# Two operand sums in other places of VectorE's row, one cast from VectorE to ScalarE, one copy from GpSimd to ScalarE

## The chip, the core and the metric

The kernel runs on one core of a Trainium2 chip. The engines are PE (TensorE, matrix products, with its weight loads PEld), DVE (VectorE), ACT (ScalarE), POOL (GpSimd) and SP (SyncE, which here only issues transfers). Each engine works through its own list of instructions in order and waits for the others by semaphores. The metric is the device time of one launch in microseconds (us). Before the change the median of six runs is 120.89 us (120.22 to 121.39).

## The reference

```python
a: (1024, 1024)   b: (1024, 2048)   c: (2048, 1024)      # float32
h = np.matmul(a, b)
h = 0.5 * h * (1 + np.tanh(np.sqrt(2 / np.pi) * (h + 0.044715 * h ** 3)))
return np.matmul(h, c).astype(np.float32)
```

Two matrix products with a tanh-GELU between them. The hidden matrix h has 1024 rows and 2048 columns.

## The kernel before

The kernel holds the hidden matrix transposed (`hT`, two halves of 512 columns, one for each half of the rows of a), so that the first product needs a transposed: `aT`, made on PE from bfloat16 copies of a. The order of the work on every engine is written out by hand. It has four stages.

**The plain stage (`block`, L136, and `mm1`, L99).** The first 512 columns of b are multiplied in the ordinary way, while a and this part of b arrive. SP loads a in eight pieces (`load_a(h, q)`: half h of the rows, quarter q of the columns) and b in four, alternately: a(0,0), b0, a(1,0), a(0,1), b1, a(1,1), a(0,2), b2, and so on. Each piece of a goes through three steps: `cast_a` (L115) makes a bfloat16 copy `ab` on the engines that it is given, in equal parts; `turn` (L123) transposes its eight 128x128 tiles on PE into a bank of PSUM; and DVE copies the two halves of the bank into `aT` (L129). Pieces of b are cast on ACT (`cast_b`, L131). `block(h, tiles, ks)` then runs the products of half h for contraction steps ks. At the end ACT puts the eight results through GELU.

**Stage zero (`seven(zero, ...)`, L391)** computes the next 512 columns of h as a 2x2 block product with seven block multiplications in place of eight (Strassen-Winograd). Its blocks of a are `BB[k half][row half]` (L200), views of `aT`; its blocks of b are quarters of columns 512 to 1023 of `b1`. The seven products are P1, P2, P5, P6, P7, P4, P3 in the order in which they run here, with 4 contraction steps each and two output tiles each, so 8 matmuls for each product. The operands have to be made first:

- from a, on DVE: `t1` (into `t[0]`), `t2` (into `t[1]`, uses `t[0]`), `t3` (into `t[2]`) and `t4` (into `t4`, uses `t[1]`); `t[3]` is a float32r copy of `BB[1][1]`. `t1(2, 0)` is the first half of the sum (contraction steps 0 and 1 of four), `t1(2, 1)` the second. A half has 1024 elements in each of 128 partitions.
- from b, on DVE: `s1`, `s2` (uses `s1`), `s3`, `s4`; on ACT: `plain_s`, a negated copy.

P5 multiplies `s[0]` by `t[0]`, P6 `s[1]` by `t[1]`, P7 `s[2]` by `t[2]`, P4 `s[3]` by `t4`, and P3 `s4` by `t[3]`. Between the products the function `between0` (L361) puts the remaining sums into the lists: `s3` and `s4` after P2's additions, the two halves of `t4` after those. Results leave PSUM by ACT (`snap`, L277, copies a bank) and DVE (`plus`, L282, adds a bank to such a copy).

**Stage one** does the same for columns 1024 to 2047 with four tiles for each product, from `b2`, and reuses zero's sums of a. **Stage two** is the second product, also with seven multiplications, from `hT` and `c_sb`; it ends with the stores.

The buffers matter for the change. Slots `x0` to `x3` of the pool `big` are used several times. `x1` first holds the float32 quarters 0 and 1 of a (`sta[0]`), `x3` the quarters 2 and 3 (`sta[1]`). Then `pair(1)` puts `t[0]` and `t[1]` into `x1` (L227) and `pair(3)` puts `t[3]` and the home of `s[0]` into `x3` (L256). A write into a slot must wait until all casts have read what was there. `pair(2)` takes `x2`, which nothing uses earlier.

POOL issues the transfers that cast on their way: six of 512 KB for the other three quarters of b (L87, L90: the first two for `b1`, which stage zero needs, then four for `b2`), and eight of 512 KB for c (L259 and L260). They start when a(0,3) is there (`gate`, L82). In the list of POOL the two copies into `t[3]` (L258) stand between b's issues and c's.

Of the kernel before, what the change touches and what calls it, by code (L numbers as in the profile page):

```python
# [19 lines left out]
def kernel(ctx, tc, a, b, c, out):  # L20
    nc = tc.nc
# [5 lines left out]
    NT = N // 128  # L27
# [3 lines left out]
    cv = c.rearrange("(nt p) q -> p nt q", p=128)  # L31
# [8 lines left out]
    def slot(tag, shape, dt, name):  # L40
        return big.tile(shape, dt, name=name, tag=tag)

    def bank(i, shape=(128, H), dt=F32, name="ps"):
        return pp.tile(list(shape), dt, name=name, tag=f"bank{i}", padded_shape=None)

    def pieces(tag, bufs, shape, dt, name):
        return small.tile(shape, dt, name=name, tag=tag, bufs=bufs)
# [8 lines left out]
    c_sb = keep.tile([128, NT, P], BF16, name="c_sb")  # L56
# [31 lines left out]
    for n in range(2):  # L88
        for k in range(0, KT, 4):
            nc.gpsimd.dma_start(out=b2[:, k:k + 4, ts(n, H)],  # L90
                                in_=bv[:, k:k + 4, ds(1024 + n * H, H)])

    def copy(eng, dst, src):
        if eng is nc.scalar:
            nc.scalar.activation(dst, src, AF.Copy)
        else:
            nc.vector.tensor_copy(dst, src)

    def mm1(p, t, h, ks):  # L99
        for k in ks:  # L100
            nc.tensor.matmul(p, b1[:, k, ts(t, 128)], aT[:, h, k],  # L101
                             start=(k == 0), stop=(k == KT - 1))

    def gelu(t, h, p):
        nc.scalar.activation(hT[h][:, t], p, AF.Gelu_apprx_tanh)  # L105
# [9 lines left out]
    def cast_a(h, q, *engs):  # L115

        ab = pieces("ab", 2, [128, 4, 256], BF16, "ab")
        for i, eng in enumerate(engs):
            w = 256 // len(engs)
            copy(eng, ab[:, :, ts(i, w)], sta[q // 2][:, h, q % 2][:, :, ts(i, w)])  # L120
        return ab

    def turn(h, q, i, ab):  # L123
        pt = bank(i, (128, 2, H), BF16, "pt")
        for n in range(2):
            for m in range(4):
                nc.tensor.transpose(pt[:, n, ts(m, 128)], ab[:, m, ts(n, 128)], ident)  # L127
        for n in range(2):
            nc.vector.tensor_copy(aT[:, h, 2 * q + n], pt[:, n])  # L129

    def cast_b(k, n=1):  # L131
        for i in range(n):
            r = ds(i * (H // n), H // n)
            nc.scalar.activation(b1[:, k, r], stb[:, k, r], AF.Copy)  # L134

    def block(h, tiles, ks):  # L136
        for k in ks:
            for t in tiles:
                mm1(ps[h, t], t, h, (k,))
# [56 lines left out]
    def pair(i):  # L196
        x = slot(f"x{i}", [128, 2, 4, H], F32R, "x1")
        return x[:, 0], x[:, 1]

    BB = [[aT[:, 0, 0:4], aT[:, 1, 0:4]], [aT[:, 0, 4:8], aT[:, 1, 4:8]]]  # L200

    def quarters(b, c0, w):
        return [[b[:, 0:4, ds(c0, w)], b[:, 4:8, ds(c0, w)]],
                [b[:, 0:4, ds(c0 + w, w)], b[:, 4:8, ds(c0 + w, w)]]]

    zero = Seven(4, quarters(b1, H, 256), BB, [None] * 4, [None] * 4, 2)
# [11 lines left out]
    ab = cast_a(0, 1, nc.scalar, nc.scalar)  # L218
# [2 lines left out]
    block(1, range(3), (1,))  # L221
    cast_b(2)
    cast_b(3)
    ab = cast_a(1, 1, nc.vector, nc.vector)
    block(0, range(4), (2,))
    turn(1, 1, 7, ab)
    zero.t[0], zero.t[1] = pair(1)  # L227
    zero.t1(2, 0)
    block(0, range(4), (3,))
    ab = cast_a(0, 2, nc.scalar)  # L230
    cast_b(4)
# [4 lines left out]
    ab = cast_a(1, 2, nc.vector)  # L236
# [4 lines left out]
    ab = cast_a(0, 3, nc.scalar)  # L241
# [3 lines left out]
    turn(0, 3, 7, ab)  # L245
    block(1, range(3), (5,))
    ab = cast_a(1, 3, nc.scalar, nc.vector)
    zero.t1(2, 1)
    block(0, range(4), (6, 7))
    for t in range(4):  # L250
        gelu(t, 0, ps[0, t])
    ps[1, 3] = bank(7)
    mm1(ps[1, 3], 3, 1, range(2))
    turn(1, 3, 0, ab)
    mm1(ps[1, 3], 3, 1, range(2, 6))
    zero.t[3], x31 = pair(3)  # L256
    for i in (0, 2):
        nc.gpsimd.tensor_copy(zero.t[3][:, i:i + 2], BB[1][1][:, i:i + 2])  # L258
    for t in range(0, NT, 2):  # L259
        nc.gpsimd.dma_start(out=c_sb[:, t:t + 2], in_=cv[:, t:t + 2])  # L260
    zero.t[2], x21 = pair(2)
    zero.t3(2, 0)
    zero.t2(2, 1)
    zero.t3(2, 1)
    block(1, range(3), (6, 7))
# [95 lines left out]
    def between0(n):  # L361
        if n == "P1":
            zero.plain_s()
        elif n == "P2":
            zero.s3()
            zero.s4(x31[:, :, 256:])
        elif n == "P5":
            zero.t4(t4, 2)
            one.last_t = t4
# [19 lines left out]
    zero.s1()  # L389
    zero.s2()  # L390
    seven(zero, done0, between0)  # L391
    one.s[3] = slot("b1", [128, 2, 4, H], F32R, "x1")[:, 0]
    one.s1()
# [68 lines left out]
```

## Time and profile before

| what | value |
|---|---|
| median of six runs | 120.89 us (120.22 to 121.39) |
| profiled execution: its own time / its span | 121.18 us / 119.4 us |
| PE busy in the span | 112.7 us (94%), 538 matmuls |
| DVE busy | 91.3 us (76%), 106 instructions |
| ACT busy | 55.7 us (47%), 92 instructions |
| POOL busy | 14.0 us (12%), 23 instructions |
| granted clock of PE | 1.00 in all stages |
| plain stage, 0 to 26.64 us | PE 23.92, DVE 14.37, ACT 12.79 us busy |
| stage zero, 26.64 to 40.75 us (14.11 us) | PE 13.40, DVE 12.60, ACT 9.18 us busy |
| stage one, 40.75 to 65.83 us (25.08 us) | PE 25.08, DVE 19.81, ACT 17.79 us busy |
| stage two, 65.83 to 119.40 us (53.57 us) | PE 50.31, DVE 44.54, ACT 15.90 us busy |

The busy time of PE is the sum of modelled spans of pipelined matmuls, so 100% does not mean its peak. The stages are cut where the first matmul of each stage starts. The profiled execution took 1.78 us more than its span: that is what lies around it.

### The profile page before, as it was taken

The numbers are of one execution on the slowest core, as the hardware profiler recorded it, in microseconds if no ns is written. First come the engines' busy times: TensorE is split into PE (matmuls) and PEld (weight loads), VectorE is DVE, ScalarE is ACT, GpSimd is POOL, SyncE is SP. The second block draws the span as 40 slices with busy tenths as digits, with TensorE's granted clock in tenths as the row PEclk, the third lists the DMA queues.
The fourth block names the chain that finished last, engine by engine and source line by source line (L and its number), as shares of the span: only waits on it lengthen the run. The fifth ranks groups of instructions, "written<-read, shape, count | busy, mean of one in ns | idle before, by whom it ended". The sixth has DMA issues, their size and how long they took to land.

```text
span 119.4 us, 1474 instructions
## 1 busy us (share of the span) xinstructions
PE 112.7 (94%) x538; PEld 77.0 (65%) x538; DVE 91.3 (76%) x106; ACT 55.7 (47%) x92; POOL 14.0 (12%) x23
## 2 busy tenths in 40 slices
PE   6698999999998999999999999999999999999990
PEld 5453655444675644888888444488888888888860
DVE  0242497789999599980779999999999986964570
ACT  4046347569275689436669536900032992000000
POOL 2000008969332000000000000000000000000000
PEclk9999999999999999999999999999999999999999
DMA  3999999999999999999000000052000002004993
GB/s 82 291 367 364 365 353 301 184 206 207 207 206 213 210 214 210 213 210 179 3 0 0 0 5 0 0 175 88 0 0 0 0 0 93 0 21 175 365 354 139
DMA packets 13543, 17.91 MB, mean 150 GB/s; under 512 B 737, under 2 KB 8929, under 8 KB 13537
## 3 DMA queue, kind: packets, MB, share of 16 engines
q0 software_dynamic: 5344, 7.34, 35.0%
q1 hardware_dynamic: 8192, 10.49, 25.8%
q8 instruction: 4, 0.07, 0.2%
q14 instruction: 3, 0.02, 0.0%
HBM read 20.97 MB, written 4.19 MB: 211 GB/s over the span
## 4 chain that ended last, share of the span: by engine, by line
PE 81%; DVE 8%; DMA 5%; ACT 2%; issue 1%; SPq 0%; DVEq 0%
PE ps L192 66%; PE ps L101 13%; DVE x L150 6%; DMA stb<-in_b_dram 5%; PE pt L127 3%; ACT hT L105 2%; DVE ot L284 1%; DVE aT L129 0%; SPq L68 0%; DVE ot L350 0%; ACT b L134 0%; DVEq L284 0%
## 5 line engine op out<-in xcount | busy, mean ns | idle before, releaser
L192 PE MATMUL ps<-x,s 128*128 128x512 f32 x128 | 29.6, 391 | 0.0
L192 PEld LDWEIGHTS ps<-x,s 128*128 128x128 f32 x128 | 24.0, 188 | 5.1
L192 PE MATMUL ps<-x,x 128*128 128x512 f32 x96 | 22.7, 392 | 0.3 <-DVE x L150 0.3
L192 PEld LDWEIGHTS ps<-x,x 128*128 128x128 f32 x96 | 17.9, 188 | 4.5 <-ACT x L188 0.7
L101 PE MATMUL ps<-aT,b 128*128 128x512 bf16 x64 | 16.9, 408 | 0.6 <-DVE aT L129 0.5
L192 PE MATMUL ps<-c_sb,hT 128*128 128x512 bf16 (+1 forms) x72 | 14.2, 356 | 0.0
L279 ACT ACTIVATE v<-ps 128x512 f32<-128x512 f32 x10 | 6.0, 598 | 17.4 <-PE ps L192 17.4
L192 PE MATMUL ps<-x 128*128 128x512 f32 x56 | 13.6, 394 | 0.4 <-DVE x L150 0.3
L105 ACT ACTIVATE hT<-ot 128x512 bf16<-128x512 f32 x18 | 10.7, 626 | 5.4 <-DVE ot L284 5.4
L192 PEld LDWEIGHTS ps<-x 128*128 128x128 f32 x56 | 10.2, 188 | 3.5 <-DVE x L150 0.8
L284 DVE TENSOR_TENSOR ot<-ps,v 128x512 f32<-128x512 f32 x10 | 6.7, 688 | 6.4 <-DMA out_dram<-ot 3.9
L192 PEld LDWEIGHTS <-hT 128*128 128x128 bf16 x72 | 6.9, 98 | 7.0 <-issue 0.5
L129 DVE COPY aT<-pt 128x512 bf16<-128x512 bf16 x16 | 6.0, 420 | 7.0 <-PE pt L127 6.9
L101 PEld LDWEIGHTS <-b 128*128 128x128 bf16 x64 | 6.2, 103 | 7.9 <-issue 1.4
L192 PE MATMUL ps<-aT,b 128*128 128x512 bf16 x48 | 10.7, 379 | 0.0
L284 DVE TENSOR_TENSOR ot<-ps,u 128x512 f32<-128x512 f32 x10 | 6.7, 690 | 5.1 <-ACT u L279 5.1
L150 DVE TENSOR_TENSOR x<-c_sb 128x1024 fp32r<-128x1024 bf16 x8 | 9.2, 1218 | 0.0
L105 ACT ACTIVATE hT<-ps 128x512 bf16<-128x512 f32 x14 | 7.3, 596 | 2.1 <-PE ps L101 2.1
L192 PEld LDWEIGHTS <-b 128*128 128x128 bf16 x48 | 4.6, 98 | 5.7 <-issue 0.3
L279 ACT ACTIVATE u<-ps 128x512 f32<-128x512 f32 x10 | 5.9, 598 | 3.3 <-PE ps L192 3.2
L279 ACT ACTIVATE p<-ps 128x512 f32<-128x512 f32 x9 | 5.3, 599 | 3.8 <-PE ps L192 3.8
L134 ACT ACTIVATE b<-stb 128x512 bf16<-128x512 f32 (+1 forms) x9 | 4.7, 573 | 5.0 <-DMA stb<-in_b_dram 5.0
(39 smaller groups left out, 113.4 us busy)
## 6 DMA issues: line engine op xcount, KB each, us to landing
sta<-in_a_dram SPq DMA_DIRECT2D x8, 512.0 KB, 8.9
c_sb<-in_c_dram POOLq DMA_DIRECT2D x8, 512.0 KB, 19.5
b<-in_b_dram POOLq DMA_DIRECT2D x6, 512.0 KB, 10.4
out_dram<-ot SPq DMA_DIRECT2D x12, 256.0 KB, 2.1
stb<-in_b_dram SPq DMA_DIRECT2D x4, 512.0 KB, 8.7
out_dram<-ot SPq DMA_DIRECT2D x8, 128.0 KB, 2.0
```

Source lines behind the costliest of these rows:

```text
L101: nc.tensor.matmul(p, b1[:, k, ts(t, 128)], aT[:, h, k], start=(k == 0), stop=(k == KT - 1))
L105: nc.scalar.activation(hT[h][:, t], p, AF.Gelu_apprx_tanh)
L127: nc.tensor.transpose(pt[:, n, ts(m, 128)], ab[:, m, ts(n, 128)], ident)
L129: nc.vector.tensor_copy(aT[:, h, 2 * q + n], pt[:, n])
L134: nc.scalar.activation(b1[:, k, r], stb[:, k, r], AF.Copy)
L150: nc.vector.tensor_tensor(out=dst[:, r], in0=x[:, r], in1=y[:, r], op=op)
L192: nc.tensor.matmul(p[:, ds(c0, w)], l[:, k, ts(j, 128)], r[:, k, ds(c0, w)], start=(start and k == 0), stop=(k == self.kt - 1), skip_group ...
L279: nc.scalar.activation(st, p, AF.Copy)
L284: nc.vector.tensor_tensor(out=ot, in0=p, in1=st, op=ADD)
```

## The change

Five things are done. The cast of a(1,1) goes from DVE (two instructions) to ACT (two instructions). On DVE `t1(2, 0)` moves ahead of the two copies of `turn(1, 1)`, and `t1(2, 1)` takes the place that `t1(2, 0)` had. `t3(2, 0)` moves to where `t1(2, 1)` was, ahead of the last copies into `aT`. The copy into `t[3]` goes from POOL to ACT in two halves: the first between the two groups of GELUs at the end of the plain stage, the second after `plain_s` in stage zero. And c's eight issues on POOL, with no copy ahead of them any more, follow directly on b's; their lines are now L92 and L93. The number of instructions on PE and its order are the same; the lists of DVE, ACT and POOL change by -2, +4 and -2 instructions.

```diff
@@ -89,6 +89,8 @@
             nc.gpsimd.dma_start(out=b2[:, k:k + 4, ts(n, H)],
                                 in_=bv[:, k:k + 4, ds(1024 + n * H, H)])
+    for t in range(0, NT, 2):
+        nc.gpsimd.dma_start(out=c_sb[:, t:t + 2], in_=cv[:, t:t + 2])
@@ -221,11 +223,12 @@
     cast_b(2)
     cast_b(3)
-    ab = cast_a(1, 1, nc.vector, nc.vector)
+    ab = cast_a(1, 1, nc.scalar, nc.scalar)
     block(0, range(4), (2,))
-    turn(1, 1, 7, ab)
     zero.t[0], zero.t[1] = pair(1)
     zero.t1(2, 0)
+    turn(1, 1, 7, ab)
+    zero.t1(2, 1)
     block(0, range(4), (3,))
     ab = cast_a(0, 2, nc.scalar)
@@ -245,21 +248,17 @@
     block(1, range(3), (5,))
     ab = cast_a(1, 3, nc.scalar, nc.vector)
-    zero.t1(2, 1)
+    zero.t[2], x21 = pair(2)
+    zero.t3(2, 0)
     block(0, range(4), (6, 7))
     for t in range(4):
         gelu(t, 0, ps[0, t])
+    zero.t[3], x31 = pair(3)
+    zero.plain_t(2, 0)
     ps[1, 3] = bank(7)
     mm1(ps[1, 3], 3, 1, range(2))
     turn(1, 3, 0, ab)
     mm1(ps[1, 3], 3, 1, range(2, 6))
-    zero.t[3], x31 = pair(3)
-    for i in (0, 2):
-        nc.gpsimd.tensor_copy(zero.t[3][:, i:i + 2], BB[1][1][:, i:i + 2])
-    for t in range(0, NT, 2):
-        nc.gpsimd.dma_start(out=c_sb[:, t:t + 2], in_=cv[:, t:t + 2])
-    zero.t[2], x21 = pair(2)
-    zero.t3(2, 0)
     zero.t2(2, 1)
     zero.t3(2, 1)
     block(1, range(3), (6, 7))
@@ -361,6 +360,7 @@
         if n == "P1":
             zero.plain_s()
+            zero.plain_t(2, 1)
```

## The prediction

> **What bounds the kernel now.** I read the stage table first. Stage one has no gap on PE (25.08 us busy of 25.08), stage zero has one: 13.40 of 14.11. PE's timeline says where, and its waits say on whom.
>
> ```profile
> 26.64 3.62 PE L192 MATMUL ps<-aT,b 128*128 128x512 bf16 x16
> 30.53 3.87 PE L192 MATMUL ps<-x,x 128*128 128x512 f32 x16 [0.27 <-DVE x L150]
> 34.24 2.86 PE L192 MATMUL ps<-x 128*128 128x512 f32 x10
> 37.43 3.47 PE L192 MATMUL ps<-x 128*128 128x512 f32 x14 [0.34 <-DVE x L150]
> ```
>
> The columns are start, length, engine, line, operation, count, idle time and releaser. Both stops wait for DVE's sums. The listed idle times are too small, since ends are modelled; I work with starts. In P1 and P2 (16 matmuls) the first starts at 26.64 and the last ends at 30.26; with some 0.39 for one, the starts are (3.62 - 0.39)/15 = 0.215 apart, so P5 could have begun at 26.64 + 16 x 0.215 = 30.08. It began at 30.53: **0.45 lost**. P5 and P6 take (34.24 - 30.53)/16 = 0.232 each. Ten matmuls follow (8 of P7, 2 of P4), so the third of P4 could have begun at 34.24 + 10 x 0.232 = 36.56. It began at 37.43, five hundredths after the end of t4's second half (37.38): **0.87 lost**. Together 1.32 us.
>
> Stage one follows at 40.75. What DVE did in that time is the second view, with POOL's row beside it.
>
> ```profile
> 24.25 0.76 DVE L129 COPY aT<-pt 128x512 bf16<-128x512 bf16 x2 [1.06 <-PE pt L127]
> 24.92 1.22 DVE L150 TENSOR_TENSOR x<-aT 128x1024 fp32r<-128x1024 bf16 x1
> 26.06 2.06 DVE L150 TENSOR_TENSOR x<-aT,x 128x1024 fp32r<-128x1024 bf16 x1
> 28.04 1.21 DVE L150 TENSOR_TENSOR x<-aT 128x1024 fp32r<-128x1024 bf16 x1
> 29.17 1.21 DVE L150 TENSOR_TENSOR x<-b 128x1024 fp32r<-128x1024 bf16 x1
> 30.42 1.23 DVE L150 TENSOR_TENSOR x<-x,b 128x1024 fp32r<-128x1024 f32 x1
> 31.56 1.28 DVE L284 TENSOR_TENSOR ot<-ps,p 128x512 f32<-128x512 f32 x2
> 32.76 1.22 DVE L150 TENSOR_TENSOR x<-b 128x1024 fp32r<-128x1024 bf16 x1
> 33.89 1.22 DVE L150 TENSOR_TENSOR x<-b,x 128x1024 fp32r<-128x1024 bf16 x1
> 35.03 2.35 DVE L150 TENSOR_TENSOR x<-x,aT 128x1024 fp32r<-128x1024 f32 x2
> ```
> ```profile
> 25.07 1.97 POOL L258 CAST x<-aT 128x1024 fp32r<-128x1024 bf16 x1 [0.92 <-DVE aT L129]
> 26.99 3.65 POOL L260 DMA_DIRECT2D c_sb<-in_c_dram  x5
> ```
>
> From the last copy into aT on, DVE has no idle time: t3(2,0), t2(2,1), t3(2,1), s1, s2, two additions, s3, s4, t4. So whatever leaves this row ahead of s1 moves everything behind it, and P5 (needs s1) and P4 (needs t4) are what PE stops for. One sum is odd: t2's second half took 2.06, its first half, same form, 1.23 at 19.80. POOL's copy ran until 27.04 beside it.
>
> From 37.43 on the chain of waits is PE alone up to the last addition:
>
> ```profile
> 37.43 78.72 PE ps L192 x358
> 116.16 0.02 issue
> 116.18 0.42 DVE ot L350
> ```
>
> so time won before 37.43 reaches the end, if nothing later stands at a fixed time.
>
> **The change, part by part.**
>
> *t3(2,0) leaves the row behind 24.25.* It goes to 21.98, where t1's second half stood (1.22, the same length); t1's second half goes to 15.66, where its first stood, and the first to 13.67, where DVE ran the two casts of a(1,1) (0.75 for both). What is left behind 24.25 is shorter by 26.06 - 24.92 = 1.14.
>
> *POOL's copies go.* t2(2,1) should take 1.23 as its first half did: its distance to the next sum falls from 1.98 to 1.14, 0.84 less. Bounds: 0 (the stretch has another cause) and 0.84; I take 0.84, since POOL's record ends at 27.04, 1.08 before t2's end, about what is left of a sum.
>
> *A dependence appears:* t2(2,1) now follows directly on the copy that it reads. s2 behind s1 shows such a distance: 30.42 is 0.04 after s1's end (30.38), where free sums overlap by 0.08. So it starts 0.04 after the copies' end (25.01), at 25.05 and not at 24.92: 0.13 lost.
>
> DVE's row is thus earlier by 1.14 + 0.84 - 0.13 = 1.85 from t3(2,1) on: t2(2,1) at 25.05, t3(2,1) 26.19, s1 27.32, s2 28.57, additions 29.71 and 30.31, s3 30.91, s4 32.04, t4 33.18 to 35.53. Each must find its inputs. s1 reads the second of b's chunks: issued at 19.4, landed 7.6 later at 27.0, by the issue and landing times. P2's two tiles end at about 29.4 and 30.26, just ahead of their additions.
>
> *PE then:* P5 at 30.08 (s1 done 28.53); P6 at 31.94 (s2 done 29.80); P7 at 33.79 (s3 done 32.13); P4 at 35.65 (t4's first half done 34.40), its third matmul at 36.11 (second half done 35.53). Nothing waits, with 0.58 to spare at the last: 1.32 won. Since 0.58 is spare, small errors in the 1.85 don't matter.
>
> *The cast of a(1,1) on ACT* costs two of the row of a(0,1)'s, 1.15 for both. ACT was idle from 12.15 to 14.07. When does a(1,1) land? These ACT rows tell:
>
> ```profile
> 11.00 1.15 ACT L134 ACTIVATE b<-stb 128x512 bf16<-128x512 f32 x2 [0.16 <-DMA stb<-in_b_dram]
> 14.07 1.06 ACT L95 ACTIVATE ab<-sta 128x1024 bf16<-128x1024 f32 x1 [1.92 <-DMA sta<-in_a_dram]
> ```
>
> b1 is there at 11.00 and a(0,2) at 14.07, with a(1,1) between them; a(1,3) came 1.50 after b3 (19.73, 21.23). So about 12.5, and the cast ends at 13.65. There is a new wait: t1(2,0) writes slot x1, which this cast reads, so DVE stands until the cast is done, and behind it stand the copies of turn(1,1) at 14.99. DVE is free for it at 13.7; t1 then ends at about 14.95. No cost, but no reserve above some 0.1. Bounds: 0, and with a landing only just before 13.67 (where DVE's cast began without waiting) t1 would start at 14.86 and end at 16.08, 1.0 late. I take 0. The second half of t1 reads the copy ahead of it and starts some 0.1 later than 15.66; DVE had 16.88 to 16.94 idle ahead of the next copies, so at most some hundredths reach PE.
>
> *The two copies on ACT* take 1.05 each, as plain_s (same size) does. The first lies in the idle 24.79 to 25.98 between the GELU groups, 0.14 to spare. Without that cover the four GELUs and P1's snaps behind them would slip as much as it overran; the second snap ends at 29.16, and the second addition needs it at 30.31. The second goes 30.11 to 31.16; then the two GELUs (1.23) to 32.4, and P6's first snap is due at 33.53 less 0.45, 33.08. No cost; 0.7 spare.
>
> *c's eight issues* pass POOL's copies and start at 23.09 in place of 26.99. Nothing lands earlier: in one queue the last b chunk ends at 37.3 (22.4 + 14.9), and from the third issue on each waits for a b chunk in both kernels. c is first used at 63.45, the last of it has landed at 37.5 + 20 = 57.5. Cost 0. The Trainium skill speaks against early issues (SBUF — State Buffer, SBUF: two separate sides): while VectorE runs certain fast copies, GpSimd can't write the descriptors of its transfers. The rows show four issues of 0.745 (20.12 to 23.09) beside DVE casts and copies, 0.71 each with sums alone; by the rule an issue at 24.25 would stand for up to the 0.76 of the copies, by the rows for 0.04, and in both cases the queue is full until 37.3, so the sum stays.
>
> **Sum:** 121.18 - 0.45 - 0.87 = 119.86 for the profiled execution (span 118.1). That execution lay 0.29 above the median, so the median goes from 120.89 to **119.6**. Its own range is 119.2 to 120.1: 0.3 of scatter, and partial costs.
>
> **Rivals.**
> 1. *Only part of it is won.* If t2's stretch stays, 0.84 - 0.58 = 0.26 comes back: 119.8. If P4's weights waited for ACT's snap u, as the releaser in PEld's row at 36.36 says, 0.38 stays (36.48 in place of 36.10): 120.0. Against the second: the snap ended at 36.02, t4's first half at 36.25.
> 2. *a(1,1) comes late*, and 1.0 is lost in the plain stage: 120.6. Against: the 1.50 between b3 and a(1,3).
> 3. *Eaten later:* in stage two DVE has hardly a gap from 63 to 97, and t3 ends (92.57) as P7 starts; if this row doesn't move along, 120.9. Against: it starts behind an addition at 61.45 that waited for PE, so it moves with PE.
> 4. *Slower: c's transfers share with b's.* If the engines served several chunks of the queue in turn, the second b chunk, alone 2.5 us, would share with two of c's and land up to 5 us later, at 32. P2 (28.36) and s1 would stand: 3.6 more, 124.5. It is slower from a landing 2 us late on (29.0, as s1 began at 29.17). Against: with five of c's issued from 26.99 on, b's chunks still ended 2.5 apart (POOL's waits end at 32.46, 34.96, 37.49).
>
> **How the numbers follow.** Forecast 0.66; rival 1 0.10; rival 2 0.08; rival 3 0.08; rival 4 and its like 0.08. A measurement of this kernel tells 0.5% (0.6 us) from no change. Faster: 0.66 + 0.10 + half of rival 2 = 0.80. Same: 0.04 + 0.08 = 0.12. Slower 0.08. The range goes to 120.7, which takes in rival 2, and down to 119.1.
>
> **What would show it.** Right: P5 starts 16 x 0.215 after P1, no wait of PE on DVE in stage zero, t2(2,1) at 1.2, stage one at about 39.4, later stages of the same length. Wrong: a wait of PE on aT between 14 and 19, a matmul of P2 that waits for b, or a longer stage two.

## The result

| | before | after |
|---|---|---|
| median | 120.67 us (120.22 to 121.39, 38 runs) | 119.87 us (119.68 to 120.11, 17 runs) |
| ratio | | 0.9923 (95%: 0.9906 to 0.9939) |
| profiled execution: time / span | 121.18 / 119.4 us | 119.71 / 117.9 us |
| first matmul of stage zero | 26.64 us | 26.54 us |
| length of stage zero | 14.11 us | 12.73 us |
| length of stage one | 25.08 us | 25.08 us |
| length of stage two | 53.57 us | 53.55 us |

The kernel became faster, by 0.0077 x 120.67 = 0.93 us (0.74 to 1.13); the medians themselves lie 0.80 apart. 119.6 was predicted, with a gain of 1.32 us. A run more than 1.5% above the fastest of its kernel counts as slow and stands in no median or ratio here. The two profiled executions differ by 1.47 us, more than the medians: this is the riddle of the case. Where the time went is plain from the two traces. Stage zero lost 1.38 us, the other stages stayed as they were.

PE's timeline of the changed kernel in stage zero (start, length, engine, line, operation, count):

```profile
26.54 3.62 PE L194 MATMUL ps<-aT,b 128*128 128x512 bf16 x16
29.81 4.00 PE L194 MATMUL ps<-x,x 128*128 128x512 f32 x16
33.65 5.78 PE L194 MATMUL ps<-x 128*128 128x512 f32 x24
39.27 7.08 PE L194 MATMUL ps<-aT,b 128*128 128x512 bf16 x32
```

Both stops are gone: P7, P4 and P3 are one piece of 24 matmuls. DVE's timeline of the same execution:

```profile
13.79 1.22 DVE L152 TENSOR_TENSOR x<-aT 128x1024 fp32r<-128x1024 bf16 x1 [1.57 <-ACT ab L97]
14.93 0.75 DVE L131 COPY aT<-pt 128x512 bf16<-128x512 bf16 x2
...
24.94 1.22 DVE L152 TENSOR_TENSOR x<-aT,x 128x1024 fp32r<-128x1024 bf16 x1
26.09 1.22 DVE L152 TENSOR_TENSOR x<-aT 128x1024 fp32r<-128x1024 bf16 x1
27.69 1.23 DVE L152 TENSOR_TENSOR x<-b 128x1024 fp32r<-128x1024 bf16 x1 [0.39 <-ACT hT L107]
...
33.56 2.35 DVE L152 TENSOR_TENSOR x<-x,aT 128x1024 fp32r<-128x1024 f32 x2
```

t2's second half takes 1.22 in place of 2.06. s1 (27.69) is idle for 0.39 first. The releaser named there, a GELU of ACT, is hardly what it waits for: s1 reads the second chunk of b, whose landing the trace puts at 19.4 + 8.0 = 27.4; POOL's fourth issue of c, which the trace has waiting for that transfer, starts at 27.68; and in two later runs the idle time ahead of s1 is put down to the transfer. t4 ends at 35.91; the third matmul of P4 needs it at about 33.65 + 10 x 0.234 = 35.99. The reserve of 0.58 in the prediction was 0.08.

The riddle shows at the start. PE's timelines, first of the kernel before, then of the changed kernel:

```profile
7.13 3.48 PE L101 MATMUL ps<-aT,b 128*128 128x512 bf16 x8
...
14.34 0.61 PE L127 MATMUL pt<-ident,ab 128*128 128x128 bf16 x8
```
```profile
7.02 1.90 PE L103 MATMUL ps<-aT,b 128*128 128x512 bf16 x8 [0.70 <-ACT b L136]
...
13.29 0.92 PE L129 MATMUL pt<-ident,ab 128*128 128x128 bf16 x8 [0.33 <-ACT ab L97]
...
15.40 0.81 PE L103 MATMUL ps<-aT,b 128*128 128x512 bf16 x3 [0.33 <-DVE aT L131]
```

The same 8 products took 3.48 us in one execution and 1.90 in the other: 0.43 and 0.215 apart. (0.43 is called half pace from here on, 0.215 full pace.) The second execution was through with the products ahead of the transposes of a(1,1) at 12.96, had to wait there, and began them 1.05 us earlier than the first. The chain of waits of the changed kernel names on what:

```profile
3.65 8.85 DMA sta<-in_a_dram
...
12.60 1.16 ACT ab L97 x2
13.76 0.02 issue
13.79 1.22 DVE x L152
15.01 0.35 DVE aT L131
15.36 0.04 issue
15.40 0.81 PE ps L103 x3
```

a(1,1) lands at 12.5, ACT casts it, t1's first half waits for that cast, the copies into aT wait for t1, PE waits for the copies.

### The profile page after: what moved, and what is told of

Its sections match the earlier page's. It is cut to its first block, busy times and chain, and to the rows that moved or that the text cites. A ratio compares the mean times of both kernels' runs of the same rounds, so it can differ in the third digit from the quotient of the medians.

```text
span 117.9 us, 1471 instructions
## 1 busy us (share of the span) xinstructions
PE 110.6 (94%) x538; PEld 75.9 (64%) x538; DVE 90.0 (76%) x104; ACT 58.6 (50%) x96; POOL 11.0 (9%) x21
## 4 chain that ended last, share of the span: by engine, by line
PE 84%; DMA 8%; SPq 2%; DVE 2%; ACT 1%; issue 0%; ACTq 0%
PE ps L194 75%; PE ps L103 8%; DMA sta<-in_a_dram 8%; PE pt L129 2%; SPq L68 1%; SPq L72 1%; DVE x L152 1%; ACT ab L97 1%; DVE ot L349 0%; DVE aT L131 0%; ACTq L97 0%
## 5 line engine op out<-in xcount | busy, mean ns | idle before, releaser
L103 PE MATMUL ps<-aT,b 128*128 128x512 bf16 x64 | 15.6, 379 | 1.6 <-DVE aT L131 0.8
L194 PE MATMUL ps<-aT,b 128*128 128x512 bf16 x48 | 10.7, 379 | 0.0
L97 ACT ACTIVATE ab<-sta 128x512 bf16<-128x512 f32 (+1 forms) x7 | 5.0, 747 | 5.0 <-DMA sta<-in_a_dram 5.0
L152 DVE TENSOR_TENSOR x<-b 128x1024 fp32r<-128x1024 bf16 (+1 forms) x4 | 7.0, 1751 | 0.4 <-ACT hT L107 0.4
```

Source lines behind the costliest of these rows:

```text
L103: nc.tensor.matmul(p, b1[:, k, ts(t, 128)], aT[:, h, k], start=(k == 0), stop=(k == KT - 1))
L152: nc.vector.tensor_tensor(out=dst[:, r], in0=x[:, r], in1=y[:, r], op=op)
L194: nc.tensor.matmul(p[:, ds(c0, w)], l[:, k, ts(j, 128)], r[:, k, ds(c0, w)], start=(start and k == 0), stop=(k == self.kt - 1), skip_group ...
```

## The experiments

Two theories were put up. **Theory S**: the start of PE decides. The kernel before's executions are of two kinds, with PE at half pace until about 10.5 us or at full pace from 5.4 us on, and the profiled one was of the first kind; the kernel before gains from an early PE, the changed one is held by the cast of a(1,1). **Theory D**: the start does not matter; c's earlier transfers delay b's second chunk, and that costs what is missing.

**Dummy matmuls at the start: more, and fewer.**

```diff
-    stir(256, 256, 256, 128)
+    stir(256, 256, 256, 128, 128, 64)     # before_warm, after_warm
+    stir(256, 256)                        # before_cold, after_cold
```

before_warm: 

> The kernel before with two more dummy matmuls (128 and 64 columns) ahead of the first transposes, which fill PE's idle time from 4.5 to 5.5 us; nothing else. Theory S (the start of PE decides: in the profiled execution of before, PE ran its first 8 products 0.43 us apart until 10.5 us, in that of after 0.215 apart): more executions start at full pace, so the median goes from about 120.7 to the lower group of before's times, 120.3 to 120.6, and the profile shows the first 8 products in about 1.9 us and stage zero starting at 26.0 to 26.2. Theory D (the start does not matter; what is missing is lost because c's early transfers delay b's second chunk): 120.5 to 120.9 with the same spread as before.

after_warm: 

> The changed kernel with the same two more dummy matmuls. Theory S: it is held in the plain stage by the cast of a(1,1) and the sum behind it, not by PE's pace, so 119.7 to 119.9 as without them, 0.7 below before_warm. Theory D: as the changed kernel too, 119.9, but 0.8 or more below before_warm.

before_cold: 

> The kernel before with two of the four dummy matmuls (256 columns each) at the start, so that PE is idle from about 3.1 to 5.5 us. Theory S: nearly all executions start at half pace, as in the profiled one; 121.1 to 121.6. Theory D: 120.6, no more than 0.2 from before.

after_cold: 

> The changed kernel with the same two dummy matmuls. Theory S: PE then comes to the transposes of a(1,1) at about 14.3, after the cast on ACT, so the prediction's sum applies: 1.2 to 1.4 below before_cold, 119.9 to 120.3. Theory D: 0.8 to 0.9 below before_cold.

The runs of the unchanged kernel before beside these gave 120.60. before_warm: 120.63 (120.43 to 121.46), ratio 1.0011 (0.999 to 1.0033). after_warm: 119.79 (119.62 to 120.18), 0.9924 (0.9895 to 0.9953). before_cold: 121.23 (120.27 to 121.92), 1.0045 (1.0021 to 1.0069). after_cold: 120.23 (119.80 to 121.38), 0.9967 (0.9943 to 0.9991).

As a switch the extra matmuls did nothing that can be seen: 9 of 12 runs of before_warm lie below 120.8, 26 of the 31 of the kernel before beside them. But the profile of before_warm caught what the profile of before did not, an execution with PE at full pace (time 120.47):

```profile
7.01 1.90 PE L101 MATMUL ps<-aT,b 128*128 128x512 bf16 x8 [0.51 <-ACT b L134]
...
25.93 3.62 PE L192 MATMUL ps<-aT,b 128*128 128x512 bf16 x15
29.82 3.91 PE L192 MATMUL ps<-x,x 128*128 128x512 f32 x16 [0.27 <-DVE x L150]
33.57 2.82 PE L192 MATMUL ps<-x 128*128 128x512 f32 x10
36.73 3.47 PE L192 MATMUL ps<-x 128*128 128x512 f32 x14 [0.34 <-DVE x L150]
40.04 6.22 PE L192 MATMUL ps<-aT,b 128*128 128x512 bf16 x27
```

before_cold's profile is one at half pace (time 121.21):

```profile
7.05 3.59 PE L101 MATMUL ps<-aT,b 128*128 128x512 bf16 x8 [0.41 <-ACT b L134]
...
26.68 3.62 PE L192 MATMUL ps<-aT,b 128*128 128x512 bf16 x16
...
40.78 5.57 PE L192 MATMUL ps<-aT,b 128*128 128x512 bf16 x24
```

Stage zero is equally long in both (14.11, 14.10), and both stops are there. Only its start moves, by 0.75, and the time with it, by 0.74. So the kernel before has two times, about 120.5 and 121.2, by PE's pace at the start: its 38 runs lie in two groups (20 up to 120.67, 15 from 121.08, three between), and fewer dummy matmuls put 9 of 12 into the upper one, against 5 of the 31 beside them. That each of these runs belongs to its group by PE's pace is inferred; three profiled executions show it. Theory S holds for the kernel before. The changed kernel, at full pace, starts stage zero at 26.54, where before at full pace starts it at 25.93: its plain stage is 0.61 longer, stage zero 1.38 shorter, sum 0.77; the times differ by 120.47 - 119.71 = 0.76. DVE's lines show where the 0.61 arises. In before_warm the copies of turn(1,1) stand at 13.85, in the changed kernel behind t1's first half, at 14.93:

```profile
13.85 0.76 DVE L129 COPY aT<-pt 128x512 bf16<-128x512 bf16 x2 [0.49 <-PE pt L127]
```

after_cold doesn't settle its part: 1.00 below before_cold lies between the theories. In its profile (121.38) the first piece of b came to ACT 1.13 late (7.68 in place of 6.55) and the half pace lasted through the transposes behind the products (1.06 for eight, 0.66 in before_cold's). Less the 1.13 its time would be 120.25, about the median, so half pace that lasts longer may be what after_cold's executions have in common; one profile doesn't show it.

**c's transfers late.** A one-column copy on POOL, which waits for the last part of aT, stands ahead of c's issues.

```diff
-    for t in range(0, NT, 2):
-        nc.gpsimd.dma_start(out=c_sb[:, t:t + 2], in_=cv[:, t:t + 2])
...
+    nc.gpsimd.tensor_copy(g2, BB[1][1][:, 3, 0:1])
+    for t in range(0, NT, 2):
+        nc.gpsimd.dma_start(out=c_sb[:, t:t + 2], in_=cv[:, t:t + 2])
```

> The changed kernel with c's transfers issued only when the last part of aT is there (a copy of one column on POOL ahead of them), some 2 us later. The prediction costs their earlier issue at nothing: 119.8 to 119.9, and b's second chunk lands at 27.5 to 27.8 here too. If the early issues delay that chunk (theory D): it lands at 27.0 to 27.2, s1 starts at 27.3, and the time is the same or up to 0.1 less.

Measured 119.98 (119.79 to 120.27), ratio 0.9915 (0.9884 to 0.9947). c's first issue began at 26.24 in place of 23.06, and s1 waits for b's second chunk as ever. DVE's line of c_late:

```profile
27.94 1.23 DVE L151 TENSOR_TENSOR x<-b 128x1024 fp32r<-128x1024 bf16 x1 [0.54 <-DMA b<-in_b_dram]
```

Theory D falls. In the traces whose loads began as usual that chunk lands between 27.0 and 27.8, with late c's (27.0 in before, 27.5 in before_warm, 27.7 in before_cold, 27.1 in pool_back, 27.6 in c_late) and with early ones (27.4 in the changed kernel, 27.5 in after_warm, 27.8 in order, 27.2 in both). That spread belongs to the executions, not to the change.

**One part undone at a time.** pool_back puts the copy into `t[3]` back on POOL, with c's issues behind it as before, t3_back puts t3's first half back behind the last copies into aT, plain_back undoes what the change does in the plain stage.

```diff
-    for t in range(0, NT, 2):                         # pool_back
-        nc.gpsimd.dma_start(out=c_sb[:, t:t + 2], in_=cv[:, t:t + 2])
...
-    zero.plain_t(2, 0)
...
+    for i in (0, 2):
+        nc.gpsimd.tensor_copy(zero.t[3][:, i:i + 2], BB[1][1][:, i:i + 2])
+    for t in range(0, NT, 2):
+        nc.gpsimd.dma_start(out=c_sb[:, t:t + 2], in_=cv[:, t:t + 2])
...
-            zero.plain_t(2, 1)
```
```diff
-    zero.t[2], x21 = pair(2)                          # t3_back
-    zero.t3(2, 0)
...
     mm1(ps[1, 3], 3, 1, range(2, 6))
+    zero.t[2], x21 = pair(2)
+    zero.t3(2, 0)
```
```diff
-    ab = cast_a(1, 1, nc.scalar, nc.scalar)           # plain_back
+    ab = cast_a(1, 1, nc.vector, nc.vector)
     block(0, range(4), (2,))
+    turn(1, 1, 7, ab)
     zero.t[0], zero.t[1] = pair(1)
     zero.t1(2, 0)
-    turn(1, 1, 7, ab)
-    zero.t1(2, 1)
...
+    zero.t1(2, 1)
     zero.t[2], x21 = pair(2)
     zero.t3(2, 0)
```

pool_back: 

> The changed kernel with the copy into t[3] back on POOL (both halves, at their old place, c's transfers behind them). The prediction's step: t2's second half is stretched from 1.22 to 2.06 by POOL's copy beside it. If that is so: t3's second half ends at about 28.1, s1 starts 0.35 to 0.4 later than in the changed kernel, PE waits as much for t4, 120.1 to 120.3. If the stretch had another cause: 119.8 to 119.9 and 1.22 for that sum.

Measured 120.24 (119.92 to 120.32), ratio 0.9929 (0.9904 to 0.9954). DVE's line and POOL's line of pool_back:

```profile
26.15 2.06 DVE L150 TENSOR_TENSOR x<-aT 128x1024 fp32r<-128x1024 bf16 x1
```
```profile
25.04 2.10 POOL L260 CAST x<-aT 128x1024 fp32r<-128x1024 bf16 x1 [0.79 <-DVE aT L129]
```

Now it is t3's second half that takes 2.06, as it is the one that starts under POOL's copy; t2's takes 1.23. So the stretch follows the copy and not the sum. s1 began at 28.13, 0.44 later than in the changed kernel, stage zero took 13.14 (0.41 more), the median is 0.37 higher. Against c_late, run beside it on the same chip, stage zero is 0.24 longer and the median 0.26 higher. The ratio (0.9929 against 0.9923) doesn't tell the two kernels apart, since before's median beside it was 120.92, with 8 of 17 runs in the upper group (15 of 38 beside the changed kernel): it is the traces that show the stretch.

t3_back: 

> The changed kernel with t3's first half back behind the last copies into aT. The prediction's step: it adds 1.14 to DVE's row ahead of s1. Of this b's second chunk hides about 0.4 (s1 stands that long in the changed kernel): s1 at about 28.4, PE waits 0.7 for t4, 120.5 to 120.7.

Measured 120.38 (120.30 to 120.55), ratio 0.9955 (0.9936 to 0.9974); 0.51 above the changed kernel, a little less than expected (by the ratios 0.39). PE's lines, of an execution at half pace (8 products in 3.59), show the second stop back in its place; s1 began at 28.37:

```profile
33.80 2.55 PE L194 MATMUL ps<-x 128*128 128x512 f32 x10
36.63 3.47 PE L194 MATMUL ps<-x 128*128 128x512 f32 x14 [0.28 <-DVE x L152]
```

plain_back: 

> The changed kernel with its plain stage as before: the cast of a(1,1) on DVE, t1's first half behind the copies of turn(1,1), its second half together with t3's first at 21.8. The other parts of the change stay. If the new wait for ACT costs 0.5 in the plain stage and the second limit stands: stage zero starts at 25.9 to 26.3, stage one at 39.2 to 39.4, 119.7 to 120.0. If these moves are what brings the gain: 120.3 or more.

Measured 119.91 (119.57 to 121.31), ratio 0.9922 (0.9895 to 0.9949): the moves in the plain stage bring nothing by themselves. t1's second half and t3's first fit together into the gap ahead of the last copies (21.99 to 24.34). In its profile PE fell from full to half pace after the first three of the 8 products (3.06 in all), so it shows nothing of the start of stage zero at full pace.

**The two limits taken away, one by one and together.** swap exchanges the slots, so that t1 writes one that no cast reads; order makes s3, which needs b's first chunk only, ahead of s1, and t4 ahead of s4.

```diff
-    zero.t[0], zero.t[1] = pair(1)        # swap
+    zero.t[0], zero.t[1] = pair(2)
-    zero.t[2], x21 = pair(2)
+    zero.t[2], x21 = pair(1)
...
+    zero.s3()                             # order
     zero.s1()
     zero.s2()
...
-            zero.s3()
-            zero.s4(x31[:, :, 256:])
...
             zero.t4(t4, 2)
             one.last_t = t4
+            zero.s4(x31[:, :, 256:])
```

swap: 

> The changed kernel with slots x1 and x2 exchanged (t[0] and t[1] in x2, t[2] in x1), so that t1's first half no longer waits for the cast of a(1,1) on ACT. Two limits are supposed to hold the changed kernel at the same place: the plain stage (that wait) and stage zero (s1 waits for b's second chunk at about 27.7, so t4 ends at about 35.9). If both are there: t1's first half starts at about 12.1, stage zero starts at 25.9 to 26.1 in place of 26.5, but PE then waits for t4, stage one starts at 39.2 to 39.3 as before, and the time stays at 119.7 to 119.9. If only the wait for the cast holds it: 119.3.

order: 

> The changed kernel with s3 made ahead of s1 (it needs b's first chunk only) and s4 behind t4. If both limits are there: t4 ends at about 34.3 in place of 35.9, and nothing is gained, since PE comes no earlier out of the plain stage: 119.7 to 119.9. If only b's second chunk holds it: 119.3 to 119.5.

both: 

> Both edits together. If both limits are there: stage zero starts at 25.9 to 26.1, PE does not wait in it, stage one starts at 38.6 to 38.8, 119.2 to 119.4. If one of them is no limit, as much as the better of the two alone.

swap: 119.87 (119.43 to 120.12), ratio 0.9907 (0.9876 to 0.9938). order: 119.79 (119.68 to 120.84), 0.9920 (0.9894 to 0.9946). both: 119.33 (119.16 to 120.01), 0.9882 (0.9848 to 0.9916). Neither alone moves the median by 0.1, together they take 0.54 off. By the ratios, each against the kernel before beside it, it is 0.19, 0.04 and 0.49, and the intervals of swap and order take in the changed kernel's 0.9923. The times are as expected, but two of the three expected starts weren't seen: order's profile ran the 8 products at half pace (3.38), swap's fell to it after three of them (3.15), with stage zero at 26.75 and 26.65. That of both went from half to full pace among the 8 (2.99):

```profile
13.15 1.21 DVE L152 TENSOR_TENSOR x<-aT 128x1024 fp32r<-128x1024 bf16 x1
...
26.80 2.35 DVE L152 TENSOR_TENSOR x<-b 128x1024 fp32r<-128x1024 bf16 x2
...
31.52 2.35 DVE L152 TENSOR_TENSOR x<-x,aT 128x1024 fp32r<-128x1024 f32 x2
```
```profile
26.12 3.62 PE L194 MATMUL ps<-aT,b 128*128 128x512 bf16 x16
...
38.87 7.08 PE L194 MATMUL ps<-aT,b 128*128 128x512 bf16 x31
```

t1 waits for nothing, s3 and s1 run without a stop, t4 ends at 33.87 and PE never waits in stage zero (12.75). Four of the six runs of both (119.16 to 119.35) lie below all 17 of the changed kernel and below one more on record at 119.53. The other two (119.90, 120.01) are where an execution with stage zero at 26.65 would lie by an estimate from these lines (119.30 + 0.53 = 119.83), so this kernel seems to depend on PE's start again. But two of swap's six lie low too (119.43, 119.52), so the first limit alone seems to be worth some 0.2 where PE starts at full pace; how much the second one then holds back was to be seen in one more run.

swap_warm: 

> The kernel swap (t1's first half no longer waits for the cast on ACT) with the two more dummy matmuls of before_warm, so that most executions start at full pace; the profile of swap showed one that did not. If the second limit is there (s1 waits for b's second chunk): stage zero starts at 25.9 to 26.1, s1 at 27.6 to 28.0, PE waits 0.1 to 0.5 for t4's second half, stage one starts at 38.9 to 39.3 and the time is 119.4 to 119.7, above the 119.16 to 119.35 of the faster runs of both. If the first limit was the only one: no wait of PE in stage zero, stage one at 38.6 to 38.8, 119.2 to 119.3.

Measured 119.97 (119.47 to 121.09, 11 runs), ratio 0.9933 (0.9901 to 0.9966): inconclusive. Its three fastest runs (119.47 to 119.64) lie with swap's two between the changed kernel and both, as they would if each limit held something back. In the profiled execution (121.09) the first piece of b reached ACT at 7.87 in place of 6.55, and PE, idle for 2.47, began at half pace again:

```profile
8.35 3.55 PE L103 MATMUL ps<-aT,b 128*128 128x512 bf16 x8 [2.47 <-ACT b L136]
```

The second limit by itself is seen where b's chunk came late: s1 began at 27.78 in after_warm and at 27.94 in c_late, and stage zero took 12.95 and 12.90 there, 0.2 more than the 12.73 with s1 at 27.69. How the two share the 0.54 at full pace stays open, as no profile caught swap or order in such an execution.

## Why the prediction was right, and where its size was off

*What bounds stage zero* was right: both stops of PE were DVE's sums, and with DVE's row earlier they are gone. 1.32 was predicted for them and 1.38 measured (14.11 to 12.73). Two small errors nearly cancel: P5 began 3.27 after P1, not 16 x 0.215 = 3.44, and P5 and P6 then took 0.240 for a matmul, not 0.232.

*The parts of the 1.85.* t3's first half, 1.14: shown by t3_back. There s1 began 4.08 after the last copies into aT (28.37 - 24.29); in the changed kernel, without the wait for b, it could have begun 3.08 after them (26.09 + 1.14 - 24.15). The difference of 1.00 is the 1.14 less the dependence of 0.13. POOL's copy, 0.84 (2.06 to 1.22): shown by pool_back. The dependence, 0.13: t2's second half began 0.03 after the copies' end (24.91), as said.

*s1 at 27.32* failed: it waited to 27.69. The prediction took the chunk's landing, 27.0, from one execution as if it were fixed; it varies by 0.8. In the profiled execution it cost nothing, as the reserve of 0.58 was there for it, but it used it up; in after_warm and c_late, with s1 0.1 to 0.25 later, it cost 0.2.

*The sum against the median* is the step that was mis-sized. The prediction noted that its execution lay 0.29 above the median and subtracted the same gain from both. But that execution was of another kind than most: PE at half pace to 10.5. The rows for it stood in the profile of before, 8 products in 3.48 where 16 of the same kind took 3.62 later, and were not read. For an execution at half pace the sum seems to hold. No profile caught the changed kernel itself in one, but three variants whose medians differ from its own by less than 0.1, swap, order and plain_back, came to stage zero as late as the kernel before in its profile (26.65 to 26.75, there 26.64) and took 119.86, 119.91 and 119.80, that is 1.27 to 1.38 below 121.18. The mean granted clock that is on record for each run says the same: the six runs of the kernel before at 0.986, the value of swap's profile, took 121.14 to 121.42, and the one of the changed kernel took 119.85. Not all fits: at that value one run each of order (120.84) and plain_back (121.31) stands out, and after_cold lies only 1.00 below before_cold. At full pace the gain was 0.76. The median of before mixes both, and 0.93 lies between. That 119.6 came so close to 119.87 was partly luck: the median of six runs, 120.89, lay 0.22 above that of 38, and 120.67 less 1.32 would have been 119.35.

*The cast of a(1,1), "no cost, but no reserve"*: here the difference is lost. a(1,1) came when estimated (12.50) and ACT's cast ended at 13.76 (13.65 predicted). What was wrong is the time by which it was needed: the reserve was counted against the transposes at 14.34 and their copies at 14.99, the places of an execution at half pace. At full pace PE was there at 12.96, the copies ran at 14.93 where before_warm has them at 13.85, and the plain stage is 0.61 longer than before's. The prediction had named this as a sign that it is wrong, a wait of PE on aT between 14 and 19: it stands at 15.40. That the wait for the cast, with t1 ahead of the copies, costs the whole 0.61 is read from the chain; the runs that take it away, swap and plain_back, were not profiled at full pace. So rival 2's place was right and its reason (a late transfer) wrong.

*The two copies on ACT* cost nothing, as said: the first lay at 24.55 to 25.63 between the GELU groups (the next began at 25.88), the second at 29.91 to 30.96, and P6's first snap still waited 0.90 for PE. *c's early issues* cost nothing: c_late. Nor did they stand beside VectorE's copies: three took 2.17 from 23.06 on, across the copies at 24.15 to 24.91. What rivals 1, 3 and 4 rest on did not occur; stage two is 0.02 shorter.

## What to carry to other kernels

Before a sum is made against a profile, look whether its execution is like the others: two groups in the times, or the same matmuls at two paces within one trace, say that it may not be. Reserves must be counted against the earliest arrival that occurs, not against the arrival in that one trace: a wait that costs nothing behind a late engine is the limit when the engine is early. And when two limits end at nearly the same time, an edit that removes one shows little; here it took both to win another 0.54 us.

## What the runs showed of the hardware

PE's pace at the start differs between executions of the same program: 0.43 us for a 128x512 bfloat16 product until about 10.5 us (before), or 0.215 from 7.0 us on (the changed kernel), and the first transposes take 1.03 or 0.62 for eight. There is a third course: in swap and plain_back the transposes at 5.2 us took 0.62, PE was idle for 1.0 us, and after three products at 0.215 the rest took 0.43, until about 11 us. The granted clock in the profile's rows shows the fall and not the slow start: it reads 0.50 from 8 to 11 us in swap and plain_back, and 1.00 throughout in before, before_cold, after_cold, order and t3_back, whose products ran at half pace too. The Trainium skill (TensorE: Matmul & The Clock Gate, Part 1: The HAM clock gate) describes such a thing: PE's clock is halved until it has been busy for a window of about 3.4 us, and the windows run freely, so that the moment of the change varies from launch to launch. Its figures for 512 columns, 0.427 and 0.216 us, are the rows' 0.43 and 0.215. That the phase of such a window decides here isn't shown; that fewer dummy matmuls make the half pace more frequent (9 of 12 runs in the upper group) agrees with it, that more of them did not make it rarer doesn't speak for it.

A POOL copy from SBUF to SBUF of 1024 elements in each partition held up a sum of two SBUF operands on VectorE that began 1.0 to 1.1 us into it by 0.84 us, whichever sum that was; neither ScalarE's copy (24.55 to 25.63 beside a sum of 1.22) nor transfer issues did. The sum that ran when the copy began was not held up (24.92, 1.22), but the copy was: it took 1.97, and its first half, with VectorE nearly idle, 1.06. In c_late a copy of a single column on POOL that began 0.03 after a sum took 1.24, about as long as the sum. The rows look as if the one that begins first runs to its end while the other stands; other pairs were not tried.
